# Twenty-two additions of a fused decoder layer given to GpSimd in place of VectorE

## The chip, the cores and the metric

The kernel runs on one core of one Trainium2 chip. That core has TensorE (PE, matrix products into PSUM, with PEld for its weight loads), VectorE (DVE), ScalarE (ACT), GpSimd (POOL) and SyncE (SP, which issues loads). Each engine works through a queue of its own, in order. The metric is the device time of one execution in microseconds, as the median of several runs; lower is better.

## What is computed

One layer of a model, on 1024 positions of 1024 channels in float32. Cut to what this change touches:

```python
u = rms_norm(h, norm1_g)
z_pool, z_lru, z_gelu, z_gate = split(u @ w_in)
y_pool = causal_multiscale_pool(z_pool, pool_w, pool_scale) @ pool_proj
y_lru = rglru_branch(z_lru, z_gelu, ...) @ lru_proj
gates = sigmoid(z_gate + b_gate)
merged = gates[0] * y_pool + gates[1] * y_lru     # the addition of the pooling branch
h = h + merged @ w_out
v = rms_norm(h, norm2_g)                          # second norm: sum of h*h over the channels
h = h + (silu(g_ff) * u_ff) @ w_ffn_out           # g_ff, u_ff = split(v @ w_ffn_in)
ple_gate = sigmoid(rms_norm(h, ple_norm_g) @ w_ple_gate)   # third norm
h = h + ple_gate * (p @ w_ple_proj)
return rms_norm(h, final_g)
```

## The kernel before

Activations stand transposed: a tile is 128 channels by 1024 positions, so a tensor of 1024 channels is eight tiles. Every product is taken in float32 accuracy by three passes: an operand x is cast to a short form by ACT (`hi`, L113) and the rest x minus that is made by DVE (`lo`, L117); both stand in one tile, and TensorE adds three partial products (L217 to L219). The large products (w_in, w_out, w_ffn_in, w_ffn_out) use a seven-product Strassen scheme, whose weight sums (L192) and operand sums (L396 to L402) are DVE work too. Weight operands are called `w`; their second half is made by DVE up to three units of work ahead of the unit that uses it. Operands of activations are called xB.. and xT.. (v, g and h below are activations before that split).

The order of all engines' instructions is the order in which the program is written; nothing reorders it. `drive()` goes through units of TensorE work; before each it emits the post-processing of the unit before, the weight casts, and some of a background list.

Three places matter here.

- `done_lru` (L925 to L935), called once for each of the eight channel tiles m of the product with lru_proj: DVE multiplies the two PSUM banks with the gate (L928) and adds the pooling branch's gated tile (L929). The result g is an operand of the product with w_out.
- `residual` (L962 to L979), called for each of the eight tiles of the product with w_out: DVE adds the product z to the residual (L965), POOL issues the store of h (`store`, L86), DVE scales h to v (L969), and `add_square` (L318) lets ACT square h into `sq` (L323) and DVE add it to the sum `ss` (L324); for the first tile ACT writes `ss` itself (L320). The queue then goes on with a weight operand w (L117) and weight sums (L192). When all eight are in, `Rstd.sums` (L335) takes eight small products of ss with a vector of 1/D on TensorE (L341), three units into the product with w_ffn_in.
- `done_fout` (L1089 to L1096), called for each of the eight tiles when the product with w_ffn_out ends: two casts on ACT (L131), two scaled subtractions on DVE (L133), and `add_square` as above, into ss3. Its sums stand in TensorE's queue after three units of the product with w_ple_gate (L225).

In the region of the last two, DVE also adds PSUM banks to SBUF tiles (L495, L499, L503 into z, L1074 into h). Those read one operand from PSUM and one from SBUF; L117, L133, L192, L324, L965 and L969 read two tensors from SBUF.

Of the kernel before, what the change touches and what calls it, by code (L numbers as in the profile page):

```python
# [62 lines left out]
def hybrid_block(ctx: ExitStack, tc: tile.TileContext, xT, pT, vec, w_in, w_rgig, w_pool,  # L63
                 w_pproj, w_lru, w_out, w_fin, w_fout, w_pg, w_pp, outT):
    nc = tc.nc
    act, dve, pool, pe = nc.scalar, nc.vector, nc.gpsimd, nc.tensor
# [7 lines left out]
    def at(name, dt=F32):  # L74
        return ap_.tile([P, T], dt, name=name, tag="a", bufs=NA)
# [9 lines left out]
    def store(out, x):  # L85
        pool.dma_start(out, x)  # L86
# [20 lines left out]
    def col(base, i):  # L107
        return cv[:, base + i:base + i + 1]
# [19 lines left out]
    def split_scaled(x, scale, name):  # L128
        ops = at(name, F32R), at(name, F32R)
        for op, s in zip(ops, (LOW, HIGH)):  # L130
            act.activation(op[:, :H], x[:, s], AF.Copy, scale=scale)  # L131
        for op, s in zip(ops, (LOW, HIGH)):
            dve.scalar_tensor_tensor(op[:, H:], x[:, s], scale, op[:, :H].bitcast(F32), ALU.mult,  # L133
                                     ALU.subtract)
        return ops
# [179 lines left out]
        after()  # L315


    def add_square(x, ss, first):  # L318
        if first:
            act.activation(ss, x, AF.Square)  # L320
        else:
            sq = at("sq")
            act.activation(sq, x, AF.Square)  # L323
            dve.tensor_add(ss, ss, sq)  # L324

    class Rstd:

# [130 lines left out]
    def some_operands(acts, k, names):  # L458

        for name in names:  # L460
            if name == "T2":
                acts.run("T1", k, 0)
                acts.run("T1", k, 1)
            acts.run(name, k, 0)
            yield {"T1": 0.7, "T2": 1.4, "T4": 0.7}.get(name, 0.1)
            yield None
            acts.run(name, k, 1)
            yield 0.7
# [69 lines left out]
    state = {}  # L538

    def ple_unit(m):  # L540
# [19 lines left out]
        def pre():  # L560
            if 1 <= m <= KD // 2:
                for k in (2 * m - 2, 2 * m - 1):
                    add_square(xk[k], ss1, k == 0)
# [304 lines left out]
    t0 = {}  # L868
# [56 lines left out]
    def done_lru(m, banks):  # L925
        g = gate_of.pop(8 + m)
        for b, s in zip(banks, (LOW, HIGH)):
            dve.tensor_mul(g[:, s], g[:, s], b)  # L928
        dve.tensor_add(g, g, t0.pop(m))  # L929
        if m % 2 == 0:  # L930
            ma.a[m // 2] = g
            background.append(some_operands(ma, m // 2, ("B11", "T1")))
        else:
            ma.b[m // 2] = g
            background.append(some_operands(ma, m // 2, ("T2", "B21")))  # L935

    plain([w_lru[m] for m in range(KD)], KD, lambda: ys, done_lru, pre_lru, 2)


# [22 lines left out]
    def residual(m):  # L962
        def then(z):
            h = xr.pop(m)
            dve.tensor_add(h, h, z)  # L965
            store(h_spill[m], h)

            v = at("v")
            dve.scalar_tensor_tensor(v, h, col(C_G2, m), state["rep1"], ALU.mult, ALU.mult)  # L969
            if m % 2 == 0:  # L970
                va.a[m // 2] = v
                background.append(some_operands(va, m // 2, ("B11", "T1")))
            else:
                va.b[m // 2] = v
                background.append(some_operands(va, m // 2, ("T2",)))
            add_square(h, state["ss2"], m == 0)
            if m == KD - 1:
                state["norm2"] = Rstd(state["ss2"])
        return then  # L979
# [72 lines left out]
    hs, v2 = {}, {}  # L1052
# [32 lines left out]
    def some_v2():  # L1085
        while complete:
            done_fout(complete.popleft())

    def done_fout(m):  # L1089
        if "ss3" not in state:  # L1090
            state["ss3"] = at("ss")
            first = True
        else:
            first = False
        v2[m] = split_scaled(hs[m], col(C_G3, m), "v2")
        add_square(hs[m], state["ss3"], first)  # L1096


    chunks = [Loaded(f_spill, "f", k0, k1 - k0, [(n, k) for n in ORDER for k in range(k1 - k0)],
# [2 lines left out]
    def next_chunk(c):  # L1102

        def last(q, j, size):
            if c < len(CHUNKS):
                chunks[c].load_some()
                return
            if q == QS[3]:
                have.add("room")
            if "room" in have and complete:  # L1110
                done_fout(complete.popleft())
        return last
# [168 lines left out]
```

## Time and profile before

| | |
|---|---|
| median of 3 runs | 1430.58 us (1429.86 to 1434.26) |
| profiled execution | 1431.25 us, its span 1429.5 us |
| PE | 1368.5 us busy, 96% of the span |
| DVE | 1075.0 us, 75%, 1583 instructions |
| ACT | 697.5 us, 49% |
| POOL | 86.5 us, 6%, 194 instructions |
| granted TensorE clock | 0.976 of full speed on average |
| L929, DVE 128x1024 | 8 times, 1225 ns each, from 493.8 to 564.5 us |
| L324, DVE 128x1024 | 21 times, 1224 ns each: 7 of them near 15, 7 from 606 to 674, 7 from 1295 to 1321 us |

The span runs from the first to the last instruction; the time has 1.75 us more around it. A busy PE says little alone, since matmuls are pipelined and overlap; what counts is where PE stands idle and who releases it. An instruction's duration on DVE overlaps the next by about 0.08 us, so the step from start to start (0.60 us for 128x512, 1.14 us for 128x1024) is what one takes of the queue.

### The profile page before, as it was taken

To read this page: it belongs to the slowest core of one execution; us is meant where nothing else is said; L and a number is where in the kernel's file an instruction comes from. 1 tells how busy PE (TensorE), PEld (TensorE's weight loads), DVE (VectorE), ACT (ScalarE), POOL (GpSimd) and SP (SyncE) were. 2 spreads that over 40 slices of the span, in tenths; PEclk is the share of its full clock that TensorE was granted. 3 is DMA by queue.
4 is the path that set the end of the run, shared out by engine and by line. 5 is a ranking of instruction groups with operands and counts; after the bars stand their busy time and mean duration, and the time that the engine had idled before them with its cause. 6 is when DMAs were issued, how large, how long until landed. Compare 5 with 4: busy or idle time off the path is not lost.

```text
span 1429.5 us, 16481 instructions
## 1 busy us (share of the span) xinstructions
PE 1368.5 (96%) x5958; PEld 1119.8 (78%) x5958; DVE 1075.0 (75%) x1583; ACT 697.5 (49%) x1114; POOL 86.5 (6%) x194
## 2 busy tenths in 40 slices
PE   8899999999999999977999999999999999999986
PEld 5687888888788888756888888888888877887865
DVE  4976788888775566778798888888787866768566
ACT  6557665877866122442654444444454522126331
POOL 1003010000000000000001010111110100000000
PEclk9899999999999999988999999999999999999997
DMA  9122243332559220332024444444567798823203
GB/s 339 45 77 79 75 153 110 120 125 107 191 184 380 88 89 31 116 131 105 16 83 153 147 156 154 162 162 162 191 233 264 277 419 311 335 74 118 73 17 118
DMA packets 65026, 220.56 MB, mean 154 GB/s; under 512 B 7344, under 2 KB 9904, under 8 KB 64944
## 3 DMA queue, kind: packets, MB, share of 16 engines
q1 hardware_dynamic: 46224, 151.80, 30.0%
q0 software_dynamic: 18576, 67.64, 11.7%
q8 instruction: 47, 0.77, 0.2%
q14 instruction: 35, 0.29, 0.1%
q10 hardware_dynamic: 144, 0.06, 0.0%
HBM read 147.65 MB, written 71.83 MB: 154 GB/s over the span
## 4 chain that ended last, share of the span: by engine, by line
PE 72%; DVE 9%; ACT 4%; issue 3%; DMA 3%; DVEq 0%; ACTq 0%; SPq 0%; POOL 0%; POOLq 0%
PE ps L219 20%; PE ps L217 20%; PE ps L218 20%; PE ps L225 11%; DMA wr<-w_fout 2%; DVE w L117 1%; DVE wr L192 1%; DVE ss L324 1%; DVE v L969 1%; DVE xr L965 1%; DMA lT<-fT 1%; ACT w L113 1%; DVE pg L1145 1%; PE ps L363 1%; DVE xT L117 1%
## 5 line engine op out<-in xcount | busy, mean ns | idle before, releaser
L113 ACT CAST w<-wr 128x512 fp32r<-128x512 f32 (+2 forms) x384 | 227.0, 609 | 360.1 <-DVE wr L192 263.7
L117 DVE TENSOR_TENSOR w<-wr,w 128x512 fp32r<-128x512 f32 (+2 forms) x384 | 256.5, 672 | 49.3 <-ACT w L113 48.5
L219 PE MATMUL ps<-xT,w 128*128 128x512 f32 x704 | 277.6, 394 | 10.6 <-DVE w L117 10.6
L218 PE MATMUL ps<-xT,w 128*128 128x512 f32 x704 | 277.4, 394 | 5.8 <-DVE xT L117 5.8
L217 PE MATMUL ps<-xT,w 128*128 128x512 f32 x704 | 277.3, 394 | 0.1
L218 PE MATMUL ps<-xB,w 128*128 128x512 f32 x528 | 207.9, 394 | 9.1 <-DVE xB L117 9.0
L217 PE MATMUL ps<-xB,w 128*128 128x512 f32 x528 | 207.4, 393 | 2.7 <-ACT xB L113 1.7
L219 PE MATMUL ps<-xB,w 128*128 128x512 f32 x528 | 207.3, 393 | 0.0
L219 PEld LDWEIGHTS ps<-xT,w 128*128 128x128 f32 x704 | 134.0, 190 | 40.8 <-DVE w L117 13.2
L218 PEld LDWEIGHTS ps<-xT,w 128*128 128x128 f32 x704 | 134.1, 190 | 35.7 <-DVE xT L117 7.7
L217 PEld LDWEIGHTS ps<-xT,w 128*128 128x128 f32 x704 | 134.0, 190 | 28.6 <-ACT w L113 0.5
L218 PEld LDWEIGHTS ps<-xB,w 128*128 128x128 f32 x528 | 100.3, 190 | 32.5 <-DVE xB L117 11.8
L217 PEld LDWEIGHTS ps<-xB,w 128*128 128x128 f32 x528 | 100.1, 190 | 24.4 <-ACT xB L113 2.1
L219 PEld LDWEIGHTS ps<-xB,w 128*128 128x128 f32 x528 | 100.1, 190 | 21.1 <-DVE w L117 0.7
L225 PE MATMUL ps<-y,w 128*128 128x512 f32 x384 | 87.2, 389 | 0.0
L225 PEld LDWEIGHTS ps<-y,w 128*128 128x128 f32 x384 | 72.1, 188 | 14.9
L1074 DVE TENSOR_TENSOR h<-h,ps 128x512 f32<-128x512 f32 x68 | 46.5, 684 | 42.8 <-PE ps L219 42.6
L192 DVE TENSOR_TENSOR wr<-wr 128x512 f32<-128x512 f32 (+1 forms) x112 | 76.0, 679 | 3.1 <-DMA wr<-w_fout 1.2
L217 PE MATMUL ps<-lT,w 128*128 128x512 f32 x176 | 69.0, 392 | 2.8 <-DMA lT<-fT 2.7
L219 PE MATMUL ps<-lT,w 128*128 128x512 f32 x176 | 68.7, 390 | 0.0
L218 PE MATMUL ps<-lT,w 128*128 128x512 f32 x176 | 68.5, 389 | 0.0
L113 ACT CAST w<-s 128x512 fp32r<-128x512 f32 (+1 forms) x56 | 34.3, 613 | 60.6 <-DVE s L192 60.4
(218 smaller groups left out, 2143.6 us busy)
## 6 DMA issues: line engine op xcount, KB each, us to landing
wr<-w_fin SPq DMA_DIRECT2D x44, 512.0 KB, 5.7
fT<-xT POOLq DMA_DIRECT2D x44, 512.0 KB, 5.7
lT<-fT SPq DMA_DIRECT2D x44, 512.0 KB, 8.9
wr<-w_in SPq DMA_DIRECT2D x36, 512.0 KB, 4.3
fB<-xB POOLq DMA_DIRECT2D x33, 512.0 KB, 5.7
lB<-fB SPq DMA_DIRECT2D x33, 512.0 KB, 7.1
g<-z POOLq DMA_DIRECT2D x16, 512.0 KB, 2.9
g<-g SPq DMA_DIRECT2D x16, 512.0 KB, 6.0
```

What stands on the lines that cost most here:

```text
L113: act.copy(op[:, :x.shape[1]], x)
L117: dve.tensor_tensor(op[:, H:H + n], x, op[:, :n].bitcast(F32), ALU.subtract)
L192: f(self.place(out), self.place(a), self.place(b))
L217: pe.matmul(bank, a, xop[:, :H], start=first, stop=False, skip_group_check=more)
L218: pe.matmul(bank, a, xop[:, H:], start=False, stop=False, skip_group_check=more)
L219: pe.matmul(bank, b, xop[:, :H], start=False, stop=last, skip_group_check=more)
L225: pe.matmul(bank, w, xop[:, s], start=f, stop=e)
L324: dve.tensor_add(ss, ss, sq)
L363: pe.matmul(bank[:, i * P:(i + 1) * P], r[:, b + i:b + i + 1].broadcast_to([P, P]), ident, start=True, stop=True)
L965: dve.tensor_add(h, h, z)
L969: dve.scalar_tensor_tensor(v, h, col(C_G2, m), state["rep1"], ALU.mult, ALU.mult)
L1074: dve.tensor_add(h[t][:, s], h[t][:, s], bank)
```

## The change

`add_square` gets the engine of its addition as an argument. The calls in `residual` (second norm) and `done_fout` (third norm) pass POOL; the first norm stays on DVE. The addition in `done_lru` goes to POOL as well. That is 7 + 7 + 8 = 22 instructions; nothing is taken away or resized.

```diff
-    def add_square(x, ss, first):
+    def add_square(x, ss, first, by=dve):
         if first:
             act.activation(ss, x, AF.Square)
         else:
             sq = at("sq")
             act.activation(sq, x, AF.Square)
-            dve.tensor_add(ss, ss, sq)
+            by.tensor_add(ss, ss, sq)
...
-        dve.tensor_add(g, g, t0.pop(m))
+        pool.tensor_add(g, g, t0.pop(m))
...
-            add_square(h, state["ss2"], m == 0)
+            add_square(h, state["ss2"], m == 0, pool)
...
-        add_square(hs[m], state["ss3"], first)
+        add_square(hs[m], state["ss3"], first, pool)
```

DVE's queue at one tile of `residual` (xr is h, with the product z added; w and wr are weight operand and raw weights):

```order
@@ -548,5 +539,4 @@
 L965 TENSOR_TENSOR xr<-xr,z 128x1024
 L969 SCALAR_TENSOR_TENSOR v<-xr,cv,rstd 128x1024
-L324 TENSOR_TENSOR ss<-ss,sq 128x1024
 L117 TENSOR_TENSOR w<-wr,w 128x512
 L192 TENSOR_TENSOR wr<-wr 128x512 x2
```

The addition is gone from between v and w; the other six rounds change in the same way.

POOL's queue from the last store of `rglru` to the first stores of the feed-forward operands:

```order
 L86 DMA y_204<-ig 128x1024
+L929 TENSOR_TENSOR g<-g 128x1024 x8
 L86 DMA h_225<-xr 128x1024
 L86 DMA h_227<-xr 128x1024
+L324 TENSOR_TENSOR ss<-ss,sq 128x1024
 L86 DMA h_226<-xr 128x1024
+L324 TENSOR_TENSOR ss<-ss,sq 128x1024
 L86 DMA h_228<-xr 128x1024
+L324 TENSOR_TENSOR ss<-ss,sq 128x1024
```

The additions now stand among the stores that POOL issues, each behind the store of its own tile.

DVE's queue where the third norm's squares are taken (v is the split operand of h, h the tile to which a PSUM bank is added):

```order
 L133 SCALAR_TENSOR_TENSOR v_9931<-h,cv,v_9931 128x512
 L133 SCALAR_TENSOR_TENSOR v_9932<-h,cv,v_9932 128x512
-L324 TENSOR_TENSOR ss<-ss,sq 128x1024
 L1074 TENSOR_TENSOR h<-h,ps 128x512
 L117 TENSOR_TENSOR w<-wr,w 128x512
```

Here the instruction that follows the removed one reads PSUM (L1074). PE's and ACT's queues keep their order; the small products of ss (L341) and the casts of g wait for POOL where they waited for DVE.

## Rows read from the trace of the kernel before

**Rows 1.** Stretches: us, then busy us of each engine (instructions), granted clock, DMA.

```profile
530.00:540.00 10.00, 10.00 (x46) 8.29 (x45) 5.61 (x8) 2.28 (x4) 0.00 (x0) 1.00 0.19 54
...
620.00:630.00 10.00, 4.39 (x10) 3.47 (x11) 8.58 (x12) 4.58 (x9) 0.53 (x1) 0.57 0.30 106
```

**Rows 2.** Waits of PE from 580 to 680: total us, times, longest.

```profile
PE ps L219 <- DVE w L117: 9.2, 2, 6.2
PE ps L218 <- DVE xB L117: 8.1, 2, 7.2
```

**Rows 3.** Timeline of DVE, first stall of w_out: start, duration, instruction [idle before].

```profile
605.04 1.28 DVE L969 SCALAR_TENSOR_TENSOR v<-xr,cv,rstd 128x1024 f32<-128x1024 f32 x1
606.24 1.22 DVE L324 TENSOR_TENSOR ss<-ss,sq 128x1024 f32<-128x1024 f32 x1
607.38 0.69 DVE L117 TENSOR_TENSOR w<-wr,w 128x512 fp32r<-128x512 f32 x1
607.98 1.41 DVE L192 TENSOR_TENSOR wr<-wr 128x512 f32<-128x512 f32 x2
...
624.87 0.68 DVE L117 TENSOR_TENSOR w<-wr,w 128x512 fp32r<-128x512 f32 x1
...
628.00 0.68 DVE L117 TENSOR_TENSOR w<-s,w 128x512 fp32r<-128x512 f32 x1
```

**Rows 4.** Timeline of ACT there: the square of that round.

```profile
605.10 1.06 ACT L323 ACTIVATE sq<-xr 128x1024 f32<-128x1024 f32 x1 [2.16 <-DVE xr L965]
```

**Rows 5.** Timeline of PE: two restarts, a later step, the second norm's sums.

```profile
625.61 0.80 PE L219 MATMUL ps<-xT,w 128*128 128x512 f32 x1 [6.23 <-DVE w L117]
...
630.89 0.63 PE L219 MATMUL ps<-xT,w 128*128 128x512 f32 x1
...
668.83 0.80 PE L218 MATMUL ps<-xB,w 128*128 128x512 f32 x1 [7.20 <-DVE xB L117]
...
676.67 1.84 PE L341 MATMUL ps<-mean,ss 128*128 128x1 f32 x16
```

**Rows 6.** Timeline of DVE, second stall: its first round; the reading of the sums.

```profile
654.41 0.69 DVE L117 TENSOR_TENSOR w<-wr,w 128x512 fp32r<-128x512 f32 x1
655.01 0.68 DVE L499 TENSOR_TENSOR z<-z,ps 128x512 f32<-128x512 f32 x1
655.73 1.23 DVE L965 TENSOR_TENSOR xr<-xr,z 128x1024 f32<-128x1024 f32 x1
...
685.15 0.16 DVE L346 TENSOR_SCALAR sm<-ps 128x8 f32<-128x8 f32 x1
```

**Rows 7.** Timeline of POOL near 112: 128x8 operations (sc is a small tile).

```profile
111.95 1.24 POOL L615 TENSOR_TENSOR sc<-sc 128x8 f32<-128x8 f32 x1
...
117.98 0.49 POOL L615 TENSOR_TENSOR sc<-sc 128x8 f32<-128x8 f32 x1
...
118.87 0.20 POOL L615 TENSOR_TENSOR sc<-sc 128x8 f32<-128x8 f32 x1
```

**Rows 8.** Timeline of DVE in the same microseconds.

```profile
110.52 2.60 DVE L670 SCALAR_TENSOR_TENSOR xc<-z,cv,xc 128x1023 f32<-128x1023 f32 x2 [0.41 <-ACT xc L666]
...
117.73 0.68 DVE L117 TENSOR_TENSOR xc<-xc,xc 128x512 fp32r<-128x512 f32 x1
120.39 0.69 DVE L117 TENSOR_TENSOR w<-s,w 128x512 fp32r<-128x512 f32 x1 [1.99 <-ACT w L113]
```

**Rows 9.** Groups of POOL instructions by line: count, busy us, mean ns.

```profile
L101 POOL TENSOR_SCALAR_AFFINE_SELECT ident<-ident 128x128 f32<-128x128 f32 x1 | 0.3, 291 | 0.1
...
L98 POOL MEMSET mean<- 128x1 f32 x1 | 0.1, 98 | 0.3 <-POOLq L1273 0.3
```

**Rows 10.** Near 1309: DVE by line from 1290 to 1309, then timelines of DVE and PE.

```profile
L324 DVE TENSOR_TENSOR ss<-ss,sq 128x1024 f32<-128x1024 f32 x4 | 4.9, 1222 | 0.3 <-ACT sq L323 0.2
...
1308.30 0.68 DVE L117 TENSOR_TENSOR w<-wr,w 128x512 fp32r<-128x512 f32 x1
...
1309.04 15.72 PE L225 MATMUL ps<-v,w 128*128 128x512 f32 x68 [0.68 <-DVE w L117]
```

## The prediction, made before the changed kernel ran

> **What bounds the kernel now.** I read the busy shares first: PE is busy 96% of the span, so only a stretch in which PE stands idle can give anything, and only one in which it comes to stand idle can cost. Then I read the slices of the span and, in the three places of the change, the stretches and PE's waits. While `done_lru` runs (about 490 to 565 us), PE is busy 10.00 of 10 us and DVE 5.61 [rows 1]: TensorE is the bound, DVE has slack. While `residual` runs (596 to 676 us) it is the other way round: from 620 to 630 DVE is busy 8.58 of 10 us and PE 4.39, at a granted clock of 0.57 [rows 1], and PE waited for DVE's operands, 9.2 us for w and 8.1 us for xB [rows 2]. The reader is to see in the timelines that DVE runs its queue there instruction behind instruction: v at 605.04, the addition at 606.24, w at 607.38, weight sums at 607.98 [rows 3]. PE restarts as soon as a w or xB is done, after standing up to 6.23 and 7.20 us [rows 5]. In the third place (`done_fout`, 1289 to 1322 us) PE stands 0.68 us in all, for a w [rows 10]. So the second place decides.
>
> **What leaves DVE.** One addition takes 607.38 - 606.24 = 1.14 us of DVE's queue [rows 3]; I write h for it. Seven go in the second place, seven in the third, eight in the first.
>
> **What an addition costs on POOL.** The trace shows none of this size there. Its nearest row with a read and a write per element is the select on 128x128: 291 ns, of which a memset of one column takes 98 [rows 9]; (291 - 98) / 127 = 1.52 ns an element. 1024 elements are then 1.56 + 0.10 = 1.66 us if the second operand is read for nothing, and 3.2 us if each of the two operands takes that long. Nothing shows which; I take the middle, p = 2.4 us, and keep both ends. The Trainium skill's page GPSIMD Engine Reference, section 3.1, gives 4497 ns for this addition at 2048 elements; half of it, 2.25 us as an estimate, would make the sum below 1.2 us smaller. No run here shows that figure.
>
> **What it does to DVE meanwhile.** The small POOL operations near 112 us show that the two engines share something. Alone, a 128x8 one takes 0.20 us (at 118.87, while DVE stands idle from 118.41 to 120.39); beside a DVE instruction with two SBUF operands it takes as long as that one lasts: POOL ends at 111.95 + 1.24 = 113.19, DVE's pair ended at 113.12; POOL ends at 118.47, DVE's instruction ended at 118.41 [rows 7, 8]. So POOL stands until DVE's instruction is over and then gets its turn at once. Whether DVE likewise stands until a long POOL instruction is over, no row shows, since 8 elements are too few to see it. I take it that it does, as the nearest thing to what the rows show: whoever has the shared path keeps it to the end of its instruction. [...] By that rule the change trades h for p wherever DVE is the bound, and the sum is the one that follows; without it the sum is that of the first rival.
>
> **First place, `done_lru`.** Eight times DVE gives up 1.14 us and may stand 2.4 us for the next operand split. PE takes nothing from DVE there at once: it is busy throughout, DVE idles about 4 of 10 us [rows 1], and the operands of w_out are first needed behind 565 us. Cost and gain 0. If that cover were gone, it would be p - h = 1.3 us at each of eight.
>
> **Second place, `residual`.** In a round the square is done at 605.10 + 1.06 = 606.16 [rows 4]. DVE is still in v, and without the addition starts w at 606.24 at its heels; w ends near 606.92, POOL gets the path, and the two-operand weight sums stand until 606.92 + p instead of starting at 607.98 [rows 3]. So each round moves what follows by p - 1.06 = +1.34 us, but the w ahead of it by only the rounds before, less h.
> - First stall. The restart at 625.61 hangs on the third round's w (624.87) [rows 3, 5]: two rounds in, one more addition gone, 2 x 1.34 - 1.14 = +1.54. Behind it the w of 628.00 comes three rounds later, 628.00 + 4.02 + 0.69 = 632.71, and PE, which used it at 630.89, wants it at 632.43: +0.3 more. Together +1.84. After that DVE catches up; PE brings the rest of the stage along by that much.
> - Second stall. Its first round has L499 between w (654.41) and the next 128x1024 addition (655.73) [rows 6]; L499 reads PSUM, so 0.60 us of POOL's turn lies beside it. Three rounds come before the xB that releases PE at 668.83 [rows 5]: 3 x 1.34 - 0.6 = +3.4. The fourth, +1.34, I count in full: PE's sums at 676.67 [rows 5] need that very addition, and DVE stands late with the first operands of w_ffn_in behind it.
>
> Sum of the second place: 1.84 + 3.4 + 1.34 = +6.6; as a function of p it is 6p - 7.8, so +2.1 at p = 1.66 and +11.4 at 3.2. The stores of h that now queue behind an addition on POOL are not read before w_ffn_out and cost nothing.
>
> **Third place, `done_fout`.** Four additions lie ahead of the w of 1308.30, whose end released PE at 1309.04 [rows 10]. After three of them DVE's next instruction is L1074, which reads PSUM: POOL's turn costs p - 0.60 and saves h, +0.66 each; the fourth only saves. 3 x 0.66 - 1.14 = +0.84. At best PE's wait of 0.68 goes, at p = 3.2 it is +3.2. The third norm's sums come behind three long units of PE, and I price POOL's last addition at 0 there; were those units shorter, it would be at most p.
>
> **Sum.** +6.6 + 0.8 = +7.4 us. Against its own execution that is 1431.25 + 7.4 = 1438.7; this execution stands 0.67 above the median of the runs, so against the median 1430.58 + 7.4 = **1438.0 us**, 0.5% slower. With the ends of p it is +1.4 to +14.6: 1432 to 1445.
>
> **Rivals.**
> 1. *POOL's addition costs DVE nothing.* Then the plan works: three additions leave the path in front of the restart at 625.61 and three in front of that at 668.83, 6 x 1.14 = 6.8, and the 0.68 of the third place: -7.5. PE would also stand for a shorter time. From 625.61 to 630.89 it made 12 steps of 0.44 us at a clock near half [rows 1, 5], where later 68 took 15.72, 0.23 each [rows 10]: 12 x 0.21 = 2.5 us, and about as much behind 668.83, of which some 4 us in all could come back. 1423.1, down to 1419. For it: DVE's instructions near 112 show no lengthening [rows 8]. Against it: those POOL instructions were tiny.
> 2. *POOL starves.* DVE's back-to-back instructions keep the path, and a long addition, which may need many turns, is done only in DVE's gaps. DVE then gains its 6.8, but PE's sums at 676.67 wait for POOL, and all of PE's queue with them. DVE stops of itself only where it reads those sums, in the trace at 685.15, 8.5 us behind PE's 676.67 [rows 5, 6]. From there POOL needs p for one addition owed, 9.6 us for four: PE would stand 8.5 + 2.4 = 11 to 18 us, less the 6.8. It decides once that wait is over 7 us: +3 to +11, 1434 to 1442. For it: POOL stood 1.24 us for a job of 0.20 [rows 7]. Against it: it got its turn behind each single DVE instruction.
> 3. *They share at a finer grain*, or POOL's turns fall in DVE's idle gaps, so that DVE loses about what it saves: -4 to +4, 1427 to 1434.
>
> That the 22 instructions do leave DVE's queue, the order of the changed program shows, so this is no rival.
>
> **How the numbers follow.** Chances: forecast 0.56, rival 1 0.22, rival 2 0.12, rival 3 0.10. A measurement of this kernel tells 0.3%, 4.3 us, from no change. Faster holds rival 1: 0.22. Within: rival 3, the part of the forecast with p under about 1.9 (0.10) and the low end of rival 2 (0.04): 0.24. Slower: the rest, 0.54. The forecast's own range is 1432 to 1445. For 8 in 10 I leave out its outermost end and the lower part of rival 1: 1421 to 1444.
>
> **What would show it.** Right: POOL's additions at 1.7 to 3.2 us each; a DVE instruction with two SBUF operands behind w that lasts, or starts, about p late; PE's waits for w and xB from 596 to 690 longer by some 6 us in all, none new around 490 to 565. Wrong: DVE's instructions at their old 0.69 and 1.22 us beside POOL's, and PE's waits shorter by 3 us in each stall (rival 1); PE standing at L341 for POOL (rival 2). A lower granted clock alone, with the same waits, would be neither.

## The result: 0.6% slower

The changed kernel took 1440.27 us (median of 7 runs, 1434.47 to 1442.23) where the kernel before took 1430.58: a ratio of 1.0061, 95% interval 1.0047 to 1.0076, or +8.7 us (+6.7 to +10.9); the two medians by themselves lie 9.7 us apart. Its profiled execution took 1440.27 us, with a span of 1438.6. The prediction was 1438.0, slower.

The page of the changed kernel, first its busy engines, then from its groups of POOL (count, busy us, mean ns, idle before):

```profile
PE 1371.3 (95%) x5958; PEld 1120.5 (78%) x5958; DVE 1091.6 (76%) x1561; ACT 697.8 (49%) x1114; POOL 146.6 (10%) x216
```

```profile
L324 POOL TENSOR_TENSOR ss<-ss,sq 128x1024 f32<-128x1024 f32 x14 | 37.5, 2681 | 172.5 <-ACT sq L323 172.5
...
L929 POOL TENSOR_TENSOR g<-g 128x1024 f32<-128x1024 f32 x8 | 22.0, 2748 | 101.3 <-DVE g L928 93.1 <-issue 8.2
```

DVE runs 22 instructions fewer than before (1583 to 1561), yet is busy 16.6 us longer (1075.0 to 1091.6). A bare count says work was taken off it; its time says that the remaining instructions got longer. Which ones, the first stall of `residual` shows. Timelines of the changed kernel, POOL and then DVE (start, duration, instruction, idle before):

```profile
605.60 2.87 POOL L324 TENSOR_TENSOR ss<-ss,sq 128x1024 f32<-128x1024 f32 x1 [0.47 <-ACT sq L323]
...
614.78 2.34 POOL L324 TENSOR_TENSOR ss<-ss,sq 128x1024 f32<-128x1024 f32 x1 [0.37 <-ACT sq L323]
```

```profile
605.54 0.69 DVE L117 TENSOR_TENSOR w<-wr,w 128x512 fp32r<-128x512 f32 x1
606.14 3.61 DVE L192 TENSOR_TENSOR wr<-wr 128x512 f32<-128x512 f32 x2
...
614.84 2.83 DVE L117 TENSOR_TENSOR w<-wr,w 128x512 fp32r<-128x512 f32 x1
617.59 1.41 DVE L192 TENSOR_TENSOR wr<-wr 128x512 f32<-128x512 f32 x2
```

In the first round DVE's w started 0.06 us ahead of POOL. It kept its 0.69, and the two weight sums behind it took 3.61 where they took 1.41 before [rows 3]: 2.20 more. In the second round POOL started 0.06 us ahead of w, so w itself was held: 2.83 against 0.69, 2.14 more, and the weight sums kept their 1.41. So an addition on POOL holds DVE for about 2.2 us and saves it 1.14. POOL's own 2.87 is 0.53 longer than its 2.34 in the second round; that fits the time it stands behind w, which ends at 606.23.

An instruction that reads PSUM isn't held. In the second stall POOL's addition ran from 655.11 on; DVE:

```profile
655.11 2.88 POOL L324 TENSOR_TENSOR ss<-ss,sq 128x1024 f32<-128x1024 f32 x1 [0.44 <-ACT sq L323]
```

```profile
655.64 0.68 DVE L499 TENSOR_TENSOR z<-z,ps 128x512 f32<-128x512 f32 x1
656.35 2.72 DVE L965 TENSOR_TENSOR xr<-xr,z 128x1024 f32<-128x1024 f32 x1
```

L499 has its old 0.68 [rows 6] in the middle of it; L965, with two SBUF operands, takes 2.72 instead of 1.23.

PE then restarts later. Its timeline in the changed kernel at the places of [rows 5], with the steps just before and between them:

```profile
600.46 0.50 PE L218 MATMUL ps<-xT,w 128*128 128x512 f32 x1 [2.41 <-DVE xT L117]
...
617.72 0.79 PE L219 MATMUL ps<-xT,w 128*128 128x512 f32 x1 [5.84 <-DVE w L117]
...
625.85 0.50 PE L219 MATMUL ps<-xT,w 128*128 128x512 f32 x1 [2.64 <-DVE w L117]
...
631.15 0.80 PE L217 MATMUL ps<-xT,w 128*128 128x512 f32 x1 [1.84 <-ACT z L493]
...
663.81 0.50 PE L218 MATMUL ps<-xB,w 128*128 128x512 f32 x1 [2.25 <-DVE xB L117]
...
672.98 0.80 PE L218 MATMUL ps<-xB,w 128*128 128x512 f32 x1 [8.21 <-DVE xB L117]
...
681.55 1.84 PE L341 MATMUL ps<-mean,ss 128*128 128x1 f32 x16
```

and the partners of three of these in the kernel before, which stand in no earlier row:

```profile
601.17 0.79 PE L218 MATMUL ps<-xT,w 128*128 128x512 f32 x1 [2.40 <-DVE xT L117]
...
616.35 0.50 PE L219 MATMUL ps<-xT,w 128*128 128x512 f32 x1 [2.94 <-DVE w L117]
...
660.67 0.50 PE L218 MATMUL ps<-xB,w 128*128 128x512 f32 x1 [0.87 <-DVE xB L117]
```

The changed execution came to this place 0.71 us early (600.46 against 601.17), which is added to each difference. PE is then late by 2.08 at 617.72, 0.95 at 625.85, 3.85 at 663.81, 4.86 at 672.98 and 5.59 at the sums. Ahead of the third place it is 6.6, by the same step of PE in the kernel before and in the changed one:

```profile
1296.31 0.39 PE L217 MATMUL ps<-lB,w 128*128 128x512 f32 x1
```

```profile
1302.16 0.39 PE L217 MATMUL ps<-lB,w 128*128 128x512 f32 x1
```

PE's waits from 580 to 690 us (total, times, longest) answer to [rows 2]:

```profile
PE ps L218 <- DVE xB L117: 10.5, 2, 8.2
PE ps L219 <- DVE w L117: 8.5, 2, 5.8
PE ps L217 <- ACT z L493: 1.8, 1, 1.8
```

The wait for w is shorter than before (9.2), that for xB longer (8.1), that for z, a PSUM bank which ACT still had to empty, is new (ACT came to it late, behind a cast of v that waited for DVE). From 600.46 to the sums PE takes the same 224 steps in both kernels, and its stops on the way add up to 17.2 us before (2.94, 6.23, 0.87, 7.20) and to 21.0 after (5.84, 2.64, 1.84, 2.25, 8.21 and one of 0.24): +3.8 of the 5.59. The other 1.8 us are PE's own steps: 45 of the 224 take over 0.3 us, against 36 before. Behind the stop of 5.84 us the granted clock was 0.50 (the lower of the two levels, 1.2 GHz; 617.5 to 622.5 us), where at the same steps of the kernel before, behind a stop of 2.94, it was 1.00 (616 to 620 us). The changed kernel, then the one before, at the same two steps, 0.43 us apart and 0.23:

```profile
618.31 0.63 PE L217 MATMUL ps<-xT,w 128*128 128x512 f32 x1
618.74 0.63 PE L218 MATMUL ps<-xT,w 128*128 128x512 f32 x1
```

```profile
616.69 0.39 PE L217 MATMUL ps<-xT,w 128*128 128x512 f32 x1
616.92 0.39 PE L218 MATMUL ps<-xT,w 128*128 128x512 f32 x1
```

The third place, timelines of POOL, DVE and PE:

```profile
1300.99 2.40 POOL L324 TENSOR_TENSOR ss<-ss,sq 128x1024 f32<-128x1024 f32 x1 [157.11 <-ACT sq L323]
1303.74 2.47 POOL L324 TENSOR_TENSOR ss<-ss,sq 128x1024 f32<-128x1024 f32 x1 [0.35 <-ACT sq L323]
1306.44 2.55 POOL L324 TENSOR_TENSOR ss<-ss,sq 128x1024 f32<-128x1024 f32 x1 [0.23 <-ACT sq L323]
```

```profile
1301.31 2.64 DVE L117 TENSOR_TENSOR w<-wr,w 128x512 fp32r<-128x512 f32 x1
1303.87 5.67 DVE L133 SCALAR_TENSOR_TENSOR v<-h,cv,v 128x512 fp32r<-128x512 f32 x2
1309.46 0.67 DVE L1074 TENSOR_TENSOR h<-h,ps 128x512 f32<-128x512 f32 x1
```

```profile
1310.28 0.77 PE L217 MATMUL ps<-lT,w 128*128 128x512 f32 x1 [2.51 <-DVE h L1074]
1310.84 0.63 PE L218 MATMUL ps<-lT,w 128*128 128x512 f32 x1
1311.27 0.63 PE L219 MATMUL ps<-lT,w 128*128 128x512 f32 x1
```

Three additions come one behind the other, a square of ACT apart (2.7 us), and hold w and both subtractions L133 (5.67 for a pair that takes 1.42 elsewhere). L1074, which empties a PSUM bank, stands behind that pair, and PE stood 2.51 us for the bank. In place of the 0.68 for w [rows 10], which is gone, that is +1.8; the seven steps behind the stop take up to 0.43 us each (1310.84 to 1311.27) instead of the 0.23 of [rows 10], some 1.4 more; the granted clock was 0.50 there (1310 to 1313 us). PE's lateness grows by 3.1 here (without the 0.71, from 5.85 to 8.98 at the third norm's sums, 1333.59 against 1324.61), and little after that: 9.1 at the end, by the two spans.

In the first place PE stays at 10.00 of 10 us (the row answers to the first of [rows 1]):

```profile
530.00:540.00 10.00, 10.00 (x46) 8.29 (x45) 6.44 (x7) 2.29 (x4) 2.72 (x1) 1.00 0.18 54
```

### The profile page after: what moved, and what is told of

Read it like the earlier page. It is cut to its first block, busy times and chain, and to the rows that moved or that the text cites. A ratio compares the mean times of both kernels' runs of the same rounds, so it can differ in the third digit from the quotient of the medians.

```text
span 1438.6 us, 16518 instructions
## 1 busy us (share of the span) xinstructions
PE 1371.3 (95%) x5958; PEld 1120.5 (78%) x5958; DVE 1091.6 (76%) x1561; ACT 697.8 (49%) x1114; POOL 146.6 (10%) x216
## 4 chain that ended last, share of the span: by engine, by line
PE 72%; DVE 10%; ACT 4%; issue 3%; DMA 1%; DVEq 0%; ACTq 0%; POOL 0%; SPq 0%; POOLq 0%
PE ps L219 20%; PE ps L217 20%; PE ps L218 20%; PE ps L225 11%; DVE w L117 2%; DVE wr L192 1%; DVE xr L965 1%; DMA wr<-w_fout 1%; DMA lT<-fT 1%; ACT w L113 1%; DVE xT L117 1%; DVE v L969 1%; DVE pg L1145 1%; PE ps L363 1%; ACT pg L1143 0%
## 5 line engine op out<-in xcount | busy, mean ns | idle before, releaser
L117 DVE TENSOR_TENSOR w<-wr,w 128x512 fp32r<-128x512 f32 (+2 forms) x384 | 263.0, 689 | 47.3 <-ACT w L113 46.6
L192 DVE TENSOR_TENSOR wr<-wr 128x512 f32<-128x512 f32 (+1 forms) x112 | 84.8, 757 | 3.1 <-DMA wr<-w_fout 1.1
L1074 DVE TENSOR_TENSOR h<-h,ps 128x512 f32<-128x512 f32 x68 | 46.5, 684 | 42.6 <-PE ps L219 42.4
```

The source lines that it names most:

```text
L117: dve.tensor_tensor(op[:, H:H + n], x, op[:, :n].bitcast(F32), ALU.subtract)
L192: f(self.place(out), self.place(a), self.place(b))
L1074: dve.tensor_add(h[t][:, s], h[t][:, s], bank)
```

## The experiments

The theory: an addition on POOL shuts DVE's two-operand reads out for 2.2 us, so it costs wherever DVE is the bound. Rivals: POOL is late with the sums and PE waits for it; or one of the other two places makes the loss. Each run is set against runs of the kernel before on the same chip (their medians were 1430.7, 1430.2 and 1431.5 in three groups); brackets are 95% intervals of the ratio.

### The three places one by one

```diff
# a1_second: second norm only
+            add_square(h, state["ss2"], m == 0, pool)
# a2_third: third norm only
+        add_square(hs[m], state["ss3"], first, pool)
# a3_lru: done_lru only
+        pool.tensor_add(g, g, t0.pop(m))
```

> Only the seven additions of the second norm go to POOL; the third norm's and done_lru's stay on DVE. Theory (POOL's addition holds a path that DVE instructions with two SBUF operands need, some 2.2 us each, in exchange for 1.14 us saved): this is the second place alone, which the trace of the changed kernel puts at +6.5 us of its +9.7: 1436 to 1438 us, DVE instructions behind w or w itself at 2.7 to 3.6 us. Rival (the loss comes from consumers that wait for a slower sum or operand): the second norm's sums are the only consumer, PE never stood for them, so 1430 to 1431 us.

> Only the seven additions of the third norm go to POOL. Theory: the third place alone, +3 us: 1433 to 1434 us, with PE standing some 2.5 us near 1302 us for a bank that DVE empties late (L1074), as in the changed kernel. Rival (waiting consumers): PE's sums come three units later and did not wait, so no change, 1430 to 1431 us.

> Only the eight additions of the pooling branch go to POOL. Both theories: DVE has slack there and PE stands nowhere, so 1430 to 1431 us, within 0.1% of before, although DVE's next operand split should last 2.2 us longer at each of eight. If it is slower by over 2 us, the slack was misread; if faster by over 1 us, DVE's 1.14 us counted somewhere.

Measured: the second norm alone 1435.45, ratio 1.0033 [1.0021, 1.0046], +4.7 us; the third alone 1433.51, 1.0014 [1.0001, 1.0027], +2.0 us by the ratio (+2.8 by the medians); `done_lru` alone 1429.46, 0.9992 [0.9979, 1.0005], no change. With the second norm alone PE's waits for xB were 10.4 us, as in the changed kernel; at the sums it stood for POOL for 0.4 us:

```profile
PE ps L341 <- POOL ss L324: 0.4, 1, 0.4
```

So POOL wasn't starved, and the second place makes most of the loss. The three add up to +5.6 us where all at once gave +8.7. The intervals reach that far (each about 1.9 us to either side), so a joint effect is neither shown nor needed.

### What an addition costs as such

Three kernels leave the second norm's seven additions out, with nothing, three memsets or a one-operand POOL instruction in their place:

```diff
-            add_square(h, state["ss2"], m == 0)
# b1_none: the square is taken, the addition left out
# b2_memset
+            [pool.memset(sq, 0.0) for _ in range(3)]
# b3_one_read
+            pool.tensor_scalar(sq, sq, 1.0, None, ALU.mult)
```

> The seven additions of the second norm are left out altogether (the sum holds the first tile's squares alone); everything else is as before, on DVE. This prices the relief without POOL. Theory: three additions leave the path before each of PE's two long stalls, 6 x 1.14 = 6.8 us, and up to 4 us come back from the lower clock behind them: 1420 to 1424 us. If the relief were hidden by another wait, it would be 1428 to 1431 us, and then POOL's price in the second place would be the 6.5 us itself and not some 13.

> As with the second norm's additions left out, but in place of each POOL sets sq to zero three times: three instructions of 128x1024 that write and read nothing, about 0.9 us each by the 128x128 memset of the trace, 2.7 us together, as long as an addition. Theory (what is shared is the path by which the second SBUF operand is read): DVE is not held up, and the time is that without the additions, 1422 to 1425 us. Rival (any work of POOL's on SBUF holds DVE): as the second norm's additions on POOL, 1434 to 1438 us.

> As with the second norm's additions left out, but in place of each POOL multiplies sq by 1 in place: one 128x1024 instruction with one read and one write, which takes perhaps 1.0 to 1.6 us. Theory (POOL's reading holds the path as long as its instruction runs): a DVE instruction is held up once a round by about that time, so six times 1.0 to 1.6 us come on top of 1423 us: 1429 to 1433 us, and DVE's weight sums or w show it. Rival (only two-operand POOL instructions collide): 1422 to 1425 us.

Without the additions: 1423.06, ratio 0.9948 [0.9931, 0.9966], -7.7 us by the medians. With memsets: 1422.47, 0.9941 [0.9921, 0.9960], the same. With one operand read: 1428.12, 0.9985 [0.9972, 0.9998], a little under the expected 1429 to 1433. First POOL, then DVE in one round of the memset kernel:

```profile
604.88 2.99 POOL L979 MEMSET sq<- 128x1024 f32 x3 [0.38 <-ACT sq L323]
```

```profile
604.91 0.69 DVE L117 TENSOR_TENSOR w<-wr,w 128x512 fp32r<-128x512 f32 x1
605.51 1.41 DVE L192 TENSOR_TENSOR wr<-wr 128x512 f32<-128x512 f32 x2
```

POOL works 2.99 us beside them, longer than an addition, and DVE has its times of before. Writing doesn't hold it. The same in the kernel with one operand read:

```profile
613.34 2.84 POOL L979 TENSOR_SCALAR sq<-sq 128x1024 f32<-128x1024 f32 x1 [0.31 <-ACT sq L323]
```

```profile
613.45 1.52 DVE L117 TENSOR_TENSOR w<-wr,w 128x512 fp32r<-128x512 f32 x1
614.89 1.40 DVE L192 TENSOR_TENSOR wr<-wr 128x512 f32<-128x512 f32 x2
```

w is held by 0.83 us (1.52 against 0.69), then the weight sums run at their old pace although POOL is busy up to 616.18. The theory behind that expectation, a hold as long as POOL's instruction runs, fails here. DVE was held where POOL reads, and not where it only writes: about 0.85 us for 1024 elements of one operand, 2.2 for two. The three stand-ins also differ in the kind of operation; that the hold goes by the operands read and not by the kind fits all three but was not tried apart. PE's waits for w and xB follow: 5.1 and 4.9 us without, 5.1 and 5.0 with memsets, 7.6 and 6.7 with one operand, 8.7 and 10.4 with the addition.

### Other places for the additions, on either engine

```diff
# c1_defer_dve: the square goes into a list `late`; all seven additions later, on DVE,
# and the norm's sums behind them
+            if m0 == 4 and i in (3, 4):
+                add_late()
...
-        if q == 5 and j == 0:
+        if q == 6 or (q == 2 and j == 0):
+            add_late()
+        if q == 2 and j == 1:
...
+            state["norm2"] = Rstd(state["ss2"])
             state["norm2"].sums()
# c2_defer_pool: the same with POOL in add_late
# c5_later_sums: as c1_defer_dve, but the sums five units later
+        if q == 7 and j == 1:
```

```diff
# c3_three_dve: the first three additions where DVE waits for PE, between the stalls; four stay
+    def add_late(i, q, z):
+        if (i, q) in ((3, 6), (3, 2), (2, 7)):
+            dve.tensor_add(state["ss2"], state["ss2"], late.popleft())
# c4_three_pool: the same on POOL, behind a one-column copy of z, so that POOL waits for this place
+            pool.tensor_copy(seen[:, len(late):len(late) + 1], z[:, :1])
+            pool.tensor_add(state["ss2"], state["ss2"], late.popleft())
```

> All additions on DVE as before, but those of the second norm are issued later: three while PE works through the middle of w_out, where DVE stands idle over a microsecond at a time, four in the sixth to tenth unit of w_ffn_in, and the norm's sums behind them instead of after three units. Theory (the second place costs what DVE does between PE's restarts, nothing else): the gain of leaving them out, less what the four late ones cost in a stretch in which DVE is busy 8 to 9.9 of 10 us: 1422 to 1427 us. If DVE's lateness there reaches PE, or the later sums do: 1428 to 1432 us.

> The same later places, but the seven additions on POOL. Theory: the same 2.2 us holds fall where PE waits for nothing from DVE, so they cost little: within 2 us of the version with the late additions on DVE, 1422 to 1429 us, and 8 us or more below the same seven additions on POOL at their old place. Rival (an addition on POOL costs its price wherever it runs): 1433 to 1437 us.

> All on DVE; only the second norm's first three additions move, out of PE's first stall into three spots of DVE's queue near 636 to 645 us in which it idles 0.8 to 3.0 us; the other four and the sums stay at their places. Theory: 3 x 1.14 = 3.4 us leave the path before the restart at 625.61, some of the 2.5 us at the lower clock may come back, the gaps pay for the rest: 1424.5 to 1427.5 us.

> The same three additions at the same three spots, on POOL; there a one-column copy of the tile that DVE or ACT has just written stands ahead of each, so that POOL really waits for the moment (in the version with all seven late it did not: its additions ran as soon as the squares were there, behind the last store). Theory: a hold of 2.2 us that falls into DVE's idle 2 to 3 us, with instructions that read PSUM around it, delays nothing that PE waits for: within 1.5 us of the version with these three on DVE. Rival (POOL's price is paid wherever it runs): 3 x 2.2 us above it, less what the three no longer take on DVE: 1428 to 1431 us.

> As the version with all seven additions late on DVE (1428.7 us), but the second norm's sums another five units later, so that PE does not stand 1.9 us for the last addition there, and the spread of the result in the last but one group. Theory: those 1.9 us and the lower clock behind them come back: 1424 to 1427 us. If DVE's lateness in the first units of w_ffn_in is what costs, it stays at 1428 to 1430 us.

| | us | ratio [95%] |
|---|---|---|
| all seven later, DVE | 1428.70 | 0.9986 [0.9973, 0.9999] |
| all seven later, POOL | 1437.89 | 1.0048 [1.0032, 1.0064] |
| three between the stalls, DVE | 1427.58 | 0.9972 [0.9961, 0.9982] |
| three between the stalls, POOL | 1428.40 | 0.9986 [0.9975, 0.9997] |
| all seven later, sums later too, DVE | 1426.93 | 0.9970 [0.9956, 0.9983] |

In the first row both stalls are short (PE's waits for w 5.2 and xB 5.0 us, as without the additions), but a new wait takes part of that back, at the sums:

```profile
PE ps L344 <- DVE ss L950: 1.9, 1, 1.9
```

So the time lies in the range expected for the case that the later sums or a late DVE reach PE (1428 to 1432 us), not in that of the gain alone. With the sums five units later (last row) that wait is gone, but three shorter ones, 2.5 us in all, stand between 689 and 710 us, two for xB and one for a PSUM bank (L1028); the two rows' intervals overlap, so that the later sums gained anything is not shown.

The second row missed what was expected of it by far, and its trace says why. POOL and then DVE:

```profile
621.23 8.29 POOL L950 TENSOR_TENSOR ss<-ss,sq 128x1024 f32<-128x1024 f32 x3
...
673.17 11.03 POOL L950 TENSOR_TENSOR ss<-ss,sq 128x1024 f32<-128x1024 f32 x4
```

```profile
673.56 2.89 DVE L117 TENSOR_TENSOR w<-wr,w 128x512 fp32r<-128x512 f32 x1
676.38 5.62 DVE L192 TENSOR_TENSOR wr<-wr 128x512 f32<-128x512 f32 x2
681.93 2.83 DVE L117 TENSOR_TENSOR xT<-v,xT 128x512 fp32r<-128x512 f32 x1
```

POOL has little else to do, so an addition written later runs as soon as its operands are there and POOL's queue lets it, which was right behind a store, in the stalls again and in bursts. In a burst DVE gets one two-operand instruction per addition: four of them took 11.2 us (673.56 to 684.76). The place in the program moves an instruction against its own engine's queue only. With the copy in front, POOL did wait for the place; POOL and then DVE of that kernel:

```profile
633.94 2.40 POOL L954 TENSOR_TENSOR ss<-ss,sq 128x1024 f32<-128x1024 f32 x1
...
642.81 2.40 POOL L954 TENSOR_TENSOR ss<-ss,sq 128x1024 f32<-128x1024 f32 x1
```

```profile
635.86 0.69 DVE L498 TENSOR_TENSOR z<-z,ps 128x512 f32<-128x512 f32 x1 [3.01 <-PE ps L219]
636.46 0.69 DVE L117 TENSOR_TENSOR w<-wr,w 128x512 fp32r<-128x512 f32 x1
...
644.62 1.14 DVE L117 TENSOR_TENSOR w<-wr,w 128x512 fp32r<-128x512 f32 x1
```

The first addition lies in DVE's 3.01 us of waiting and, from 635.86 to its end at 636.34, beside L498, which reads PSUM: it holds nothing. The last holds w for 0.45 (1.14 against 0.69). So POOL can do the job for next to nothing where DVE stands anyway. But there DVE does it for nothing too, and the two came out 0.8 us apart, less than their intervals can tell. The time, 1428.40, lies in the rival's range as well (1428 to 1431); it is the trace that speaks against a price paid wherever POOL runs. What both gain is the queue ahead of the first stall, three additions shorter: PE's wait for w went from 9.2 us in two to 5.2 in one:

```profile
PE ps L219 <- DVE w L117: 5.2, 1, 5.2
```

(the kernel with three on DVE). Of the kernels that make all the additions, the two with the lowest times, 1427.58 and 1426.93 (-4.0 and -4.6 us by the medians), beat both the kernel before and the changed one, and leave all additions on DVE; the first is 0.1 above the range expected of it. Against 1423 without these additions, some 4 us are left; where they lie was not pursued.

## Why the prediction was right, and where it was not

- **The bound and the sign.** Right: in `residual` DVE is the bound, and the change trades h for p there. h = 1.14 stands: the second norm's seven additions gone gave -7.7 by the medians (-9.9 to -4.9 by the interval of the ratio), where the first rival had six of them, 6.8 us, in front of the two restarts.
- **p = 2.4.** An addition on POOL without a busy DVE lasts 2.40 us (the copy kernel), and it holds DVE for 2.14 to 2.20. The middle of the two ends is the time of the instruction and 0.2 above the hold. That it fits is luck in good part: the low end was meant for one operand read, 1.66, but a POOL instruction of this size that reads one operand lasted 2.84 us beside a busy DVE and held it for 0.83, so neither its time nor its hold goes the way the two ends were worked out. The Trainium skill's page GPSIMD Engine Reference, section 3.1, of which the prediction gave half, 2.25, lies between; these runs agree with it. At that value the prediction's sum falls by 1.4 and not by 1.2, since nine additions count in it, 0.15 each; and its 6p - 7.8 leaves the +0.3 of the first stall fixed, which moves with p as well, so the ends of the second place are +1.9 and +12.2 instead of +2.1 and +11.4.
- **Second place, +6.6.** PE's lateness shows +6.6 ahead of the third place, but the agreement is closer than its terms: first stall 2.5 (PE's arrival at the wait ahead of 663.81, 3.85 less the longer wait's 1.38) for 1.84; second stall up to 672.98 2.4 for 3.4; the rest 1.7 for 1.34. Of the first, 1.4 are stops, and these only by the new one for z (1.84), and 1.1 are slower steps of PE; no term held either. The second is all stops. Of the rest, 0.7 up to the sums are slower steps alone: PE stood for no addition there, which is what the +1.34 was counted for. So that the total came out right is in part luck. In a round in which POOL came first, w itself was held, which the forecast had not allowed. By time, with this place alone changed, it was +4.7 (3.0 to 6.6), so the term may be somewhat high.
- **Third place, +0.84: the term that was mis-sized.** It measured +3.1 in the traces and +2.0 alone. The step that failed was "After three of them DVE's next instruction is L1074": I set each addition against the instruction behind it in DVE's queue, as if POOL started there. ACT's squares set when POOL starts, and they came in a row, so w and both L133 were held. And I asked only after the w that released PE, not after the bank that L1074 empties: with DVE late, the bank became the wait that ends last.
- **First place, 0.** Right: the run with it alone shows no change, PE is never idle there, though DVE grew busier.
- **What would show it.** POOL's length (2.34 to 2.94) and the late DVE instruction came as said. "PE's waits for w and xB [...] longer by some 6 us in all" didn't: +1.7, and +3.8 with z and xT up to the sums. The rest of the lateness is in PE's steps at the lower clock.
- **Rivals.** *Costs DVE nothing* falls with the timelines and with 1.0033 for the second norm alone; its price is that of leaving the additions out. *POOL starves* falls: 0.4 us at the sums at most. *They share at a finer grain* falls for two-operand additions: each held instruction is held once, for 2.14 to 2.20 us of an addition of 2.34 to 2.40.

## What to carry to other kernels

Before work is moved to POOL, ask which DVE instructions will run beside it, and count what it reads from SBUF against what DVE saves; where DVE is the bound and reads two SBUF operands, an addition given away cost nearly twice what it saved. Look first for a place in DVE's own queue in which it waits anyway: three of these additions moved there, still on DVE, gained 4 us. An instruction on an idle engine starts when its operands are ready, so moving it in the program doesn't move it in time unless something ties it there.

## What was unexpected of the hardware

The hold follows what POOL reads, not how long its instruction lasts. Three memsets of 2.99 us held nothing, a one-operand instruction of 2.84 us held a DVE instruction for 0.83 us and let the next two run at full pace, and an addition of 2.34 us held one for 2.14. So the prediction's assumption, that whoever has the shared path keeps it to the end of its instruction, fits the addition and not the one-operand instruction. The Trainium skill's page SBUF — State Buffer, section Who interferes with whom, states that "A DVE instruction with two SBUF inputs contends with a GpSimd instruction that reads SBUF, not with one that only writes it". These traces agree on both sides: the holds of 2.14 and 0.83 us stand beside POOL instructions that read, and none beside the memsets.
